# Four matmul tasks behind each layer norm run side by side, contraction outermost

## The chip, the cores and the metric

The kernel runs on one core of a Trainium2 chip. The metric is the device time of one execution in microseconds (us). Before the change three runs gave 1962.46, 1962.93 and 1963.6 us (median 1962.93). The profiled execution took 1963.4 us, and its recorded span is 1961.5 us.

## The reference, cut to what matters

One inference step of a two-layer decoder. 592 tokens (16 meta tokens, 8 x 8 sample tokens, 512 prompt tokens) of width 1024 go through two layers. Every layer is a mixer (recurrent heads), a layer norm, a squared-ReLU MLP and a second layer norm:

```python
def _layer_norm(x, g, b):
    mu = jnp.mean(xf, -1, keepdims=True)
    var = jnp.mean(jnp.square(xf - mu), -1, keepdims=True)
    return (xf - mu) * lax.rsqrt(var + LN_EPS) * g + b

def _sq_relu_mlp(h, w1, w2):
    return jnp.square(jax.nn.relu(h @ w1)) @ w2

for layer in range(DEPTH):
    mixed, states = mixer(h, ...)             # layer 0: SSD and RG-LRU, layer 1: GLA and HGRN
    h = _layer_norm(ALPHA * h + mixed, ln1_g, ln1_b)
    h = _layer_norm(ALPHA * h + _sq_relu_mlp(h, w1, w2), ln2_g, ln2_b)
```

So there are four norms: layer 0's two, layer 1's two. What follows the first and the third is the MLP's first projection; what follows the second is layer 1's input projection (q, k, v of its first GLA head and a low-rank gate); the fourth ends the program.

## The kernel before, in words

Activations lie with the features on the partitions: 8 tiles `h` of 128 features x 592 tokens. A weight unit (`w`) is 1024 x 128: 8 contraction steps of 128 x 128. Each number is held in two float32r parts (a high one and the rest), so a step of a task is three matmuls (high x high, high x rest, rest x high), and a unit on one half of the tokens is 24 matmuls into one PSUM tile `pm` (`mm`, L175). The 592 tokens are two halves of 296 (288 in layer 1 behind its mixer). A `Task` (L263) is a unit with what consumes its two results. `run(..., by_half=True)` (L289) runs some tasks on half 0, then the same tasks on half 1. There are five `pm` banks and three `px` banks of PSUM, five weight buffers `w` and three raw buffers.

A weight unit is loaded by SyncE (SP, L120), its high part is made by ScalarE (ACT, L126) and its rest by VectorE (DVE, L127); `prep_to` (L156) issues this for units up to four ahead.

The norm (`Norm`, L397) works on the residual tiles `rs[0..7]` in halves. The last five tasks ahead of it (j = 3 to 7) run by half. After each result the residual is added on DVE (L519 or L634), `add` (L431) adds the tile to a running sum `s` on GpSimd (POOL; the eighth on DVE; L442, L444), squares it on ACT (L446) and adds the square to `ss` on DVE (L447). `finish(0)` (L449) puts the statistics of half 0 into `later`, a table of functions by contraction step, which `mm` looks up after each step: with FIK = 3 the two matmuls with ones (L463, L465) stand behind step 3 of the first task of half 1. From them come mean and 1/sigma (L466 to L474), the mean is subtracted from the eight tiles (DVE L478, POOL L480), and each tile is scaled on DVE (L494), written to `h` by ACT (L495) and its rest by DVE (L496). `finish(1)` does the same for half 1. The next tasks read the eight `h` in turn.

Behind the second norm POOL adds the bias to the eight `rs` (L645), SP stores them (L646), and behind these stores in SP's queue stand the loads of the next mixer, the small gate weight `wg2` (L1124) first; its matmuls are at L1378.

The order of the instructions on each engine is made by the framework's scheduler when the program is built: it takes what its own model of time finds ready, by priority, and fixes a list for each engine. On the chip every engine works through its list in that order.

Of the kernel before, what the change touches and what calls it, by code (L numbers as in the profile page):

```python
# [12 lines left out]
OP = mybir.AluOpType  # L13

P = 128
D = 1024
KT = 8
# [6 lines left out]
NPM = 5  # L24
NB = 5
SHK = 5
FIK = 3
FINY = (2, 4, 6)
SUBP = (1, 3, 5, 7)
KS = 8 - NB  # L30
# [41 lines left out]
def _trunk(ctx, tc, nc, I, O):  # L72
# [97 lines left out]
    def next_unit():  # L170
        u = state["use"]
        state["use"] += 1
        prep_to(u + 1 + LOOK)
        return prepped.pop(u)
# [94 lines left out]
    def drain():  # L269
        while active or later:  # L270
            for k in sorted(later):
                for fn in later.pop(k):
                    fn()
            weave()

    class Task:
# [6 lines left out]
        def half(self, i):  # L283
# [8 lines left out]
            flush()  # L292
            weave()

    def run(tasks, by_half=False, after=None):
        if by_half:
            for i in range(2):
                for t in tasks:
                    t.half(i)
                if after:  # L300
                    after(i)
        else:
            for t in tasks:
                t.half(0)
                t.half(1)
# [89 lines left out]
    class Norm:  # L395
# [3 lines left out]
        def __init__(self, new, rs, halves, gname, bname, layer, final=False):  # L399
            self.rs, self.halves, self.final = rs, halves, final  # L400
            self.gname, self.bname, self.layer = gname, bname, layer
            self.new = new

        def shift(self):

# [25 lines left out]
        def add(self, k, i):  # L431

            c0, c1 = self.halves[i]
            r = self.rs[k][:, c0:c1]
            if k == KS:
                V.tensor_tensor(r, r, self.c[:, c0:c1], OP.subtract)
            s, ss = self.s[:, c0:c1], self.ss[:, c0:c1]
            if k == 0:
                A.activation(ss, r, AF.Square)
                return  # L440
            if k == 1:
                G.tensor_tensor(s, self.rs[0][:, c0:c1], r, OP.add)  # L442
            else:
                (V if k == KT - 1 else G).tensor_tensor(s, s, r, OP.add)  # L444
            q = self.t[k % 2][:, c0:c1]
            A.activation(q, r, AF.Square)  # L446
            V.tensor_tensor(ss, ss, q, OP.add)  # L447

        def finish(self, i, dst):  # L449
            if i == 0:  # L450
                later.setdefault(FIK, []).append(lambda: step(self.finishing(i, dst)))
            else:
                drain()
                for _ in self.finishing(i, dst):
                    pass

        def finishing(self, i, dst):
            c0, c1 = self.halves[i]
            n = c1 - c0
            gname, bname, layer = self.gname, self.bname, self.layer  # L460
# [86 lines left out]
    def mlp(H, layer, halves, last, keep=None):  # L547
# [3 lines left out]
        with ExitStack() as st:  # L551
# [93 lines left out]
                        G.tensor_scalar(rs[k], rs[k], vc("ln2b", layer * 8 + k), None, OP.add)  # L645
                        nc.sync.dma_start(keep[:, k], rs[k])  # L646

            run([w1(0, f) for f in W1_ORDER[:4]], by_half=True)
            for k, f in enumerate(W1_ORDER[4:]):
                run([w1(0, f)])  # L650
                residual(2 * k)
# [467 lines left out]
    def odd_mixer(H, g):  # L1119
# [266 lines left out]
        for h in range(4):  # L1386
            q, k, v0, v1 = (g(n) for n in ("q", "k", "v", "v"))
            tasks = [copy_task(q, TAIL), copy_task(k, FULL), copy_task(v0, FULL), copy_task(v1, FULL)]
            if h == 0:
                run([Task(H, FULL, lr_consume, small=wsr[:, 1])] + tasks[0:NB], by_half=True)  # L1390
                run(tasks[NB:])
            else:
                run(tasks)
            z = [g("zs"), g("zs")]
            while len(lsg) <= h:
                weave()
            active.append(attend(q, k, lsg[h], 1.0 / 16, P ** -0.5, (v0, v1), z, hg[:, 0:2],
                                 I["gst"][h], O["gla_s"][h], O["gla_p"][h], 1))
            run([silu_task(z[0]), silu_task(z[1])])
# [209 lines left out]
```

## Time and profile before

| what | value |
|---|---|
| median of three runs | 1962.93 us |
| profiled execution, its span | 1963.4 us, 1961.5 us |
| TensorE (PE) busy | 1889.2 us, 96% of the span |
| DVE / ACT / POOL busy | 66% / 45% / 21% |
| chain that ended last | PE 81%, DVE 11%, issue 3% |
| statistics of half 0 of the four norms (L463) start at | 474.82, 886.52, 1528.01, 1930.33 us |
| statistics of half 1 (L463) start at | 499.11, 911.34, 1552.43, 1948.69 us |

Times count from the start of the span. "Busy" is the sum of the instructions' times. The clock that the power and activity control granted to TensorE is given in parts of full speed: 1.00 is 2.4 GHz, 0.50 is 1.2 GHz.

### The profile page before, as it was taken

Reading aid. Unit: us, or ns where it says so; the run is one execution under the profiler, and the core shown is the slowest. Engines: PE = TensorE matmul, PEld = TensorE weight load, DVE = VectorE, ACT = ScalarE, POOL = GpSimd, SP = SyncE. Lnnn points to the kernel's source line nnn. Section 1 sums busy time; section 2 is a strip of 40 time slices with the busy share of each in tenths; the row PEclk is TensorE's granted clock in tenths of the full one; section 3 lists DMA queues with packets and bytes.
Section 4 is the critical chain, followed back from the end, with each engine's and each line's share of the span. In section 5 each row is a group of like instructions: output and inputs, shape, how many; then the busy total and the mean of one; then the engine's idle time right before and its main releaser. Section 6 shows DMA issues by size and latency. Waiting matters only on the chain.

```text
span 1961.5 us, 33567 instructions
## 1 busy us (share of the span) xinstructions
PE 1889.2 (96%) x13854; PEld 1827.5 (93%) x13854; DVE 1299.2 (66%) x2023; ACT 885.0 (45%) x1538; POOL 408.2 (21%) x427
## 2 busy tenths in 40 slices
PE   8998899999999999998999999999999899999996
PEld 8898799899999999997899999999999899999996
DVE  7886756877875757557554456566564877575637
ACT  5333146533644444324544355565651563534333
POOL 3454432215100000135212212122112300000015
PEclk9999899999999999999999999999999999999998
DMA  6222221421213131312332322322332123131411
GB/s 202 90 103 75 78 87 55 131 77 54 87 55 118 56 118 56 118 65 86 114 111 93 107 89 88 100 79 97 102 113 76 54 76 112 61 119 55 129 54 49
DMA packets 69272, 175.96 MB, mean 90 GB/s; under 512 B 6624, under 2 KB 30304, under 8 KB 67968
## 3 DMA queue, kind: packets, MB, share of 16 engines
q1 hardware_dynamic: 69120, 173.82, 26.7%
q8 instruction: 109, 1.79, 0.4%
q14 instruction: 43, 0.35, 0.1%
HBM read 154.54 MB, written 19.25 MB: 89 GB/s over the span
## 4 chain that ended last, share of the span: by engine, by line
PE 81%; DVE 11%; issue 3%; ACT 2%; POOL 2%; DMA 0%; SPq 0%; ACTq 0%; DVEq 0%; POOLq 0%
PE pm L182 55%; PE pm L195 14%; DVE w L127 1%; DVE r L424 1%; PE px L1252 1%; PE px L1312 1%; POOL r L645 1%; PE px L1323 1%; PE px L1065 1%; PE px L1322 1%; PE px L946 1%; POOL o L1347 1%; DVE h L496 1%; DVE r L494 1%; PE px L1253 1%
## 5 line engine op out<-in xcount | busy, mean ns | idle before, releaser
L182 PE MATMUL pm<-h,w 128*128 128x296 f32 (+2 forms) x8256 | 1181.7, 301 | 12.5 <-ACT h L308 5.5
L182 PEld LDWEIGHTS pm<-h,w 128*128 128x128 f32 x8256 | 1135.9, 190 | 24.6 <-issue 5.6
L127 DVE TENSOR_TENSOR w<-raw,w 128x1024 fp32r<-128x1024 f32 (+1 forms) x300 | 370.8, 1236 | 181.9 <-ACT w L126 180.9
L126 ACT CAST w<-raw 128x1024 fp32r<-128x1024 f32 (+1 forms) x300 | 304.0, 1014 | 298.9 <-PE pm L195 148.7
L195 PE MATMUL pm<-ff,w 128*128 128x296 f32 (+1 forms) x2016 | 273.5, 297 | 0.0
L195 PEld LDWEIGHTS pm<-ff,w 128*128 128x128 f32 x2016 | 272.0, 188 | 0.3 <-DVE r L214 0.2
L620 POOL TENSOR_TENSOR sq<-sq 128x296 f32<-128x296 f32 (+1 forms) x32 | 21.5, 674 | 651.7 <-ACT sq L618 651.7
L182 PE MATMUL pm<-ff,w 128*128 128x296 f32 (+1 forms) x768 | 106.7, 301 | 0.0
L182 PEld LDWEIGHTS pm<-ff,w 128*128 128x128 f32 x768 | 105.3, 191 | 0.8 <-issue 0.3
L182 PE MATMUL pm<-m,w 128*128 128x296 f32 (+1 forms) x768 | 105.8, 299 | 0.0
L182 PEld LDWEIGHTS pm<-m,w 128*128 128x128 f32 x768 | 104.5, 189 | 0.6
L607 DVE TENSOR_TENSOR ff<-sq,ff 128x888 fp32r<-128x888 f32 (+3 forms) x48 | 58.4, 1221 | 42.2 <-ACT ff L606 42.2
L588 ACT ACTIVATE sq<-pm 128x296 f32<-128x296 f32 (+1 forms) x96 | 37.9, 415 | 87.0 <-PE pm L182 66.0
L606 ACT CAST ff<-sq 128x888 fp32r<-128x888 f32 (+3 forms) x48 | 50.3, 1050 | 39.6 <-DVE sq L601 38.9
L1347 POOL TENSOR_TENSOR o<-o,zs 128x576 f32<-128x576 f32 x16 | 30.8, 1933 | 168.1 <-DVE o L1346 168.1
L211 DVE TENSOR_TENSOR r<-r,pm 128x296 f32<-128x296 f32 (+1 forms) x96 | 43.5, 453 | 18.6 <-PE pm L195 17.9
L1265 POOL TENSOR_TENSOR sin<-sin,ebl 128x1024 f32<-128x1024 f32 (+1 forms) x12 | 29.6, 2467 | 117.9 <-issue 112.0
L589 ACT ACTIVATE sq<-sq 128x296 f32<-128x296 f32 (+1 forms) x96 | 41.2, 450 | 0.8
L1352 ACT COPY v<-pm 128x296 f32<-128x296 f32 x32 | 12.9, 405 | 60.9 <-PE pm L182 60.9
L495 ACT ACTIVATE h<-r,vec 128x296 fp32r<-128x296 f32 (+1 forms) x48 | 23.9, 536 | 34.7 <-DVE r L494 34.7
L214 DVE TENSOR_TENSOR r<-r,pm 128x296 f32<-128x296 f32 (+1 forms) x72 | 32.6, 452 | 10.2 <-PE pm L195 10.2
L618 ACT ACTIVATE sq<-pm 128x296 f32<-128x296 f32 (+1 forms) x32 | 13.1, 415 | 56.8 <-PE pm L182 53.8
(387 smaller groups left out, 2270.8 us busy)
## 6 DMA issues: line engine op xcount, KB each, us to landing
raw<-in_w_dram SPq DMA_DIRECT2D x252, 512.0 KB, 3.3
sin<-in_sst_dram SPq DMA_DIRECT2D x8, 512.0 KB, 3.6
out_ssd_s_dram<-sin SPq DMA_DIRECT2D x8, 512.0 KB, 3.1
sin<-in_gst_dram SPq DMA_DIRECT2D x4, 1024.0 KB, 7.4
out_gla_s_dram<-sin SPq DMA_DIRECT2D x4, 1024.0 KB, 3.9
sin<-in_hst_dram SPq DMA_DIRECT2D x8, 512.0 KB, 4.1
out_hgrn_s_dram<-sin SPq DMA_DIRECT2D x8, 512.0 KB, 3.5
xt<-in_x_dram SPq DMA_DIRECT2D x16, 148.0 KB, 3.9
```

The lines of the kernel that those rows point to most:

```text
L126: A.copy(w[:, 0, :n], r)
L127: V.tensor_tensor(w[:, 1, :n], r, w[:, 0, :n].bitcast(F32), OP.subtract)
L182: PE.matmul(p[:, :n], w[:, a, ks], xs[k][:, b, c0:c1], start=(k == 0 and i == 0), stop=(k == KT - 1 and i == 2))
L195: PE.matmul(p[:, :n], w[:, a, ks], xs[k][:, b, :n], start=(first and k == 0 and i == 0), stop=(k == 3 and i == 2), skip_group_check=True)
L211: V.tensor_tensor(y, y, p[:, :n], OP.add)
L214: V.tensor_tensor(y, y, p[:, :n], OP.subtract)
L588: A.activation(q, p, AF.Relu)
L589: A.activation(q, q, AF.Square)
L606: A.copy(t[:, 0, a:e, :n], s[:, a + 1:e + 1, :n])
L607: V.tensor_tensor(t[:, 1, a:e, :n], s[:, a + 1:e + 1, :n], t[:, 0, a:e, :n].bitcast(F32), OP.subtract)
L1265: G.tensor_tensor(sin, sin, ebl[:, 0:8].unsqueeze(2).to_broadcast([P, 8, N]), OP.mult)
L1347: G.tensor_tensor(o[v][:, c], o[v][:, c], gate[v][:, c], OP.mult)
```

## The change

Three things change. `together` (new, L295) runs several tasks on one half with the contraction outermost: one PSUM tile for each task, and at each step the three matmuls of every task, then the next step; the results are consumed one after the other at the end. It is used behind the first three norms. The squares are added to `ss` one tile later than before, the last of them in `finishing`. The statistics of half 0 stand behind step 6 instead of 3 (FIK), and `finish(1)` prepares one more weight unit ahead of the norm's second half.

```diff
-FIK = 3
+FIK = 6
+    def together(tasks, i):
+        ps = []
+        for t in tasks:
+            if t.small is None and t.w is None:
+                t.w = next_unit()
+            ps.append(pm())
+        for k in range(KT):
+            ks = slice(k * P, (k + 1) * P)
+            for t, p in zip(tasks, ps):
+                c0, c1 = t.halves[i]
+                if t.small is not None:
+                    ops = [(p[:32], t.small[:, k, :], b) for b in range(2)]
+                else:
+                    ops = [(p, t.w[:, a, ks], b) for a, b in ((0, 0), (0, 1), (1, 0))]
+                for j, (o, w, b) in enumerate(ops):
+                    PE.matmul(o[:, :c1 - c0], w, t.xs[k][:, b, c0:c1], start=(k == 0 and j == 0),
+                              stop=(k == KT - 1 and j == len(ops) - 1))
+            for fn in later.pop(k, ()):
+                fn()
+        for t, p in zip(tasks, ps):
+            c0, c1 = t.halves[i]
+            t.consume(p[:32 if t.small is not None else P, :c1 - c0], c0, c1, i)
+            flush()
+            weave()
             A.activation(q, r, AF.Square)
-            V.tensor_tensor(ss, ss, q, OP.add)
+            self.add_square()
+            self.square = (ss, q)
+        def add_square(self):
+            if self.square:
+                ss, q = self.square
+                V.tensor_tensor(ss, ss, q, OP.add)
+            self.square = None
             else:
+                prep_to(state["use"] + 4)
                 drain()
         def finishing(self, i, dst):
+            self.add_square()
-            run([w1(0, f) for f in W1_ORDER[:4]], by_half=True)
+            ts = [w1(0, f) for f in W1_ORDER[:4]]
+            together(ts, 0)
+            together(ts[:2], 1)
+            together(ts[2:], 1)
-                run([Task(H, FULL, lr_consume, small=wsr[:, 1])] + tasks[0:NB], by_half=True)
-                run(tasks[NB:])
+                ts = [Task(H, FULL, lr_consume, small=wsr[:, 1])] + tasks
+                together(ts[:4], 0)
+                ts[4].half(0)
+                together(ts[:2], 1)
+                together(ts[2:4], 1)
+                ts[4].half(1)
```

No instruction is added or taken away except by this: the lists of the two programs have the same lengths on each engine, and they differ only around the four norms. The line numbers of the changed kernel are higher by 26 to 40: its L311 is a matmul of `together`, L500 and L502 are the statistics (L463, L465 before), L463 is before's L436, L471 its L444, L481 its L447, L507 its L470, L515 its L478, L531 and L533 its L494 and L496, L532 its L495, L625 the MLP's Relu (L588), L1407 and L1392 the copies L1367 and L1352, L1418 its L1378.

TensorE at the start of the MLP behind the first norm, before (`pm_5260` and `pm_5294` are the results of the first two tasks on half 0, `h_4996` to `h_5003` the eight tiles, `w_4896` and `w_4930` the weights, `lns` and `lnq` the sums of half 1):

```order
L182 MATMUL pm_5260<-h_4996,w_4896 128x296 x3
L182 MATMUL pm_5260<-h_4997,w_4896 128x296 x3
L182 MATMUL pm_5260<-h_4998,w_4896 128x296 x3
L182 MATMUL pm_5260<-h_4999,w_4896 128x296 x3
L182 MATMUL pm_5260<-h_5000,w_4896 128x296 x3
L182 MATMUL pm_5260<-h_5001,w_4896 128x296 x3
L182 MATMUL pm_5260<-h_5002,w_4896 128x296 x3
L182 MATMUL pm_5260<-h_5003,w_4896 128x296 x3
L182 MATMUL pm_5294<-h_4996,w_4930 128x296
L463 MATMUL px_5192<-lns_4790,ones_78 128x296
L465 MATMUL px_5194<-lnq_4791,ones_78 128x296
```

The same place now (the eight tiles are `h_4995` to `h_5002`, the four results `pm_5260`, `pm_5266`, `pm_5272`, `pm_5278`, the fourth weight `w_5193`), the last twelve rows up to the second statistics matmul:

```order
L311 MATMUL pm_5266<-h_4996,w_4929 128x296
L311 MATMUL pm_5272<-h_4996,w_4963 128x296 x3
L311 MATMUL pm_5260<-h_4997,w_4895 128x296 x3
L311 MATMUL pm_5266<-h_4997,w_4929 128x296 x3
L311 MATMUL pm_5272<-h_4997,w_4963 128x296 x3
L311 MATMUL pm_5260<-h_4998,w_4895 128x296 x3
L500 MATMUL px_5197<-lns_4790,ones_78 128x296
L311 MATMUL pm_5266<-h_4998,w_4929 128x296 x3
L311 MATMUL pm_5272<-h_4998,w_4963 128x296 x2
L311 MATMUL pm_5278<-h_4995,w_5193 128x296
L311 MATMUL pm_5278<-h_4996,w_5193 128x296
L502 MATMUL px_5199<-lnq_4791,ones_78 128x296
```

Before, 25 matmuls of the new tasks stood ahead of L463, and they read all eight tiles; now 32 stand ahead of L500, and they read four tiles.

DVE at the end of half 1's sums of the same norm, before (L519 adds the result to the residual, `w_5257` and `w_5291` are weight rests):

```order
L519 TENSOR_TENSOR r_4553<-r_4553,pm_5163 128x296
L496 SCALAR_TENSOR_TENSOR h_5002<-r_4485,vec_73,h_5002 128x296
L496 SCALAR_TENSOR_TENSOR h_5003<-r_4553,vec_73,h_5003 128x296
L447 TENSOR_TENSOR lnq_4791<-lnq_4791,lnt_4794 128x296
L444 TENSOR_TENSOR lns_4790<-lns_4790,r_4553 128x296
L447 TENSOR_TENSOR lnq_4791<-lnq_4791,lnu_4795 128x296
L127 TENSOR_TENSOR w_5257<-raw_5255,w_5257 128x1024
L470 SCALAR_TENSOR_TENSOR lnr_4792<-px_5194,lnm_4793 128x296
L478 TENSOR_TENSOR r_4019<-r_4019,lnt_4794 128x296
```

and now:

```order
L556 TENSOR_TENSOR r_4553<-r_4553,pm_5162 128x296
L481 TENSOR_TENSOR lnq_4791<-lnq_4791,lnt_4794 128x296
L471 TENSOR_TENSOR lns_4790<-lns_4790,r_4553 128x296
L127 TENSOR_TENSOR w_5193<-raw_5191,w_5193 128x1024
L481 TENSOR_TENSOR lnq_4791<-lnq_4791,lnu_4795 128x296
L515 TENSOR_TENSOR r_4019<-r_4019,lnt_4794 128x296
L515 TENSOR_TENSOR r_4175<-r_4175,lnt_4794 128x296
L507 SCALAR_TENSOR_TENSOR lnr_4792<-px_5199,lnm_4793 128x296
L515 TENSOR_TENSOR r_4335<-r_4335,lnt_4794 128x296
L515 TENSOR_TENSOR r_4485<-r_4485,lnt_4794 128x296
L127 TENSOR_TENSOR w_5263<-raw_5261,w_5263 128x1024
L531 SCALAR_TENSOR_TENSOR r_4019<-r_4019,vec_73,lnr_4792 128x296
```

The fourth weight's rest now stands between the last addition to `lns` and the last to `lnq`, two subtractions of the mean stand ahead of the variance (L507), and a fifth weight's rest stands ahead of the scaling of half 1.

TensorE ahead of the gate weight behind the second norm, before (`pm_9525` is k on half 1, `pm_9564` and `pm_9603` the two v) ...

```order
L182 MATMUL pm_9525<-h_9062,w_8990 128x296 x3
L182 MATMUL pm_9525<-h_9063,w_8990 128x296 x3
L1378 MATMUL px_9553<-lgf_9334,wg2_9320 128x296
L1378 MATMUL px_9557<-lgf_9334,wg2_9320 128x296
L182 MATMUL pm_9564<-h_9056,w_9024 128x296 x3
```

... and now (`pm_9525` is k, `pm_9526` the first v, `pm_9603` the second v):

```order
L311 MATMUL pm_9525<-h_9062,w_8989 128x296 x3
L311 MATMUL pm_9526<-h_9062,w_9023 128x296 x3
L1418 MATMUL px_9578<-lgf_9339,wg2_9325 128x296
L1418 MATMUL px_9582<-lgf_9339,wg2_9325 128x296
L1418 MATMUL px_9592<-lgf_9339,wg2_9325 128x296
L182 MATMUL pm_9603<-h_9055,w_9252 128x296 x3
```

The 24 matmuls of the first v on half 1 stood behind the first use of the gate weight; they now stand ahead of it.

## Rows read from the trace of the kernel before

**Rows 1.** PE's waits, whole program: us in total, times, longest.

```profile
PE px L463 <- DVE ln L444: 8.1, 3, 3.5
PE px L463 <- DVE lns L444: 6.9, 2, 3.5
...
PE pm L182 <- DVE h L496: 4.6, 4, 1.4
PE px L1214 <- ACT vt L1190: 4.3, 3, 1.5
...
PE px L1378 <- DMA wg<-in_wg_dram: 3.7, 1, 3.7
```

**Rows 2.** Timeline of PE, first norm: start, us, instructions, count, idle before.

```profile
455.50 15.85 PE L182 MATMUL pm<-m,w 128*128 128x296 f32 x114
474.82 0.77 PE L463 MATMUL px<-lns,ones 128*128 128x296 f32 x2 [3.48 <-DVE lns L444]
...
499.11 1.19 PE L463 MATMUL px<-lns,ones 128*128 128x296 f32 x2
...
500.56 14.71 PE L182 MATMUL pm<-h,w 128*128 128x296 f32 x104
```

**Rows 3.** Timeline of DVE, first norm.

```profile
468.77 0.76 DVE L447 TENSOR_TENSOR lnq<-lnq,lnu 128x296 f32<-128x296 f32 x1 [0.52 <-ACT lnu L446]
...
477.78 0.46 DVE L519 TENSOR_TENSOR r<-r,pm 128x296 f32<-128x296 f32 x1 [1.12 <-PE pm L182]
...
498.15 0.45 DVE L444 TENSOR_TENSOR lns<-lns,r 128x296 f32<-128x296 f32 x1
...
498.90 1.21 DVE L127 TENSOR_TENSOR w<-raw,w 128x1024 fp32r<-128x1024 f32 x1
```

**Rows 4.** Timeline of ACT, first norm: the first Relu behind the norm's eight L495.

```profile
511.93 0.71 ACT L588 ACTIVATE sq<-pm 128x296 f32<-128x296 f32 x2
```

**Rows 5.** Timeline of PE, second norm.

```profile
925.41 2.34 PE L247 MATMUL pm<-h,wsr 128*32 128x296 f32 x16
927.59 6.77 PE L182 MATMUL pm<-h,w 128*128 128x296 f32 x48
938.07 2.34 PE L1378 MATMUL px<-lgf,wg 32*128 32x296 f32 x4 [3.71 <-DMA wg<-in_wg_dram]
940.34 5.25 PE L182 MATMUL pm<-h,w 128*128 128x296 f32 x24
945.52 1.26 PE L1378 MATMUL px<-lgf,wg 32*128 32x296 f32 x4
946.71 3.51 PE L182 MATMUL pm<-h,w 128*128 128x296 f32 x24
```

**Rows 6.** Timeline of ACT, second norm: the copy that frees the first bank.

```profile
924.98 0.38 ACT L1367 COPY lgf<-pm 32x296 f32<-32x296 f32 x1
```

**Rows 7.** Timeline of POOL, second norm.

```profile
919.38 11.90 POOL L645 TENSOR_SCALAR r<-r,vec 128x592 f32<-128x592 f32 x6 [2.17 <-DVE h L496]
...
932.03 3.51 POOL L645 TENSOR_SCALAR r<-r,vec 128x592 f32<-128x592 f32 x2
```

**Rows 8.** Timeline of SP's queue, second norm.

```profile
935.98 0.38 SPq L1124 DMA_DIRECT2D wg<-in_wg_dram  x1
```

**Rows 9.** Timeline of DVE, third norm.

```profile
1532.42 0.46 DVE L519 TENSOR_TENSOR r<-r,pm 128x288 f32<-128x288 f32 x1 [1.55 <-PE pm L182]
```

**Rows 10.** Timeline of PE, fourth norm.

```profile
1911.43 15.43 PE L182 MATMUL pm<-ff,w 128*128 128x288 f32 x114
...
1931.73 15.77 PE L182 MATMUL pm<-ff,w 128*128 128x288 f32 x108
```

**Rows 11.** Timeline of DVE, fourth norm.

```profile
1945.37 0.70 DVE L447 TENSOR_TENSOR ln<-ln 128x288 f32<-128x288 f32 x1 [0.57 <-ACT ln L446]
1947.53 0.46 DVE L634 TENSOR_TENSOR r<-r,pm 128x288 f32<-128x288 f32 x1 [1.45 <-PE pm L182]
```

**Rows 12.** PE by stretches of 2 us: length, busy (instructions), granted clock, DMA share, GB/s.

```profile
940.00:942.00 2.00, 2.00 (x8) 0.50 0.89 334
...
1932.00:1934.00 2.00, 2.00 (x9) 0.50 0.00 0
```

More of the change, by code (lines that the diff above doesn't have):

```diff
@@ L446, in add @@
             A.activation(q, r, AF.Square)
-            V.tensor_tensor(ss, ss, q, OP.add)
+            self.add_square()
[4 more added lines that the diff above has]
+                V.tensor_tensor(ss, ss, q, OP.add)
+            self.square = None
         def finish(self, i, dst):
```

## The prediction

> **What bounds the kernel now.** I read the page first: TensorE (PE) is busy for 96% of the span and is 81% of the chain that ended last, so time is won only where PE stands still, or runs at its lower clock. The list of PE's waits comes next [rows 1]. The reader is to see that the norms are most of it: 15.0 us ahead of the statistics L463 (five waits), 4.6 us for `h` from L496, 3.7 us for the gate weight `wg2`. The timelines of PE and of the engines that it waits for then say, norm by norm, what ends last.
>
> At the first norm PE stands 3.48 us ahead of L463, for the last addition to `lns` [rows 2]. The other three norms show the same wait (the list: five waits, none longer than 3.5). It is DVE that is late there: the tiles of half 0 are long done on PE. Behind it DVE works without a pause from 477.78 [rows 3] to the last sums of half 1 at 499. So the new tasks' wait for `h`, and the statistics of half 1, are set by DVE's list. Behind the second norm the wait for `wg2` has another cause: POOL's eight L645 run from 919.38 to 935.5 [rows 7], the load stands behind their stores in SP's queue [rows 8], and PE begins at 938.07 [rows 5].
>
> A wait costs more than its length. After the 3.71 us without work at 934 to 938 the granted clock was 0.50, that is 1.2 GHz [rows 12]: 24 matmuls took 5.25 us, where the next 24 took 3.51, and four L1378 took 2.34 where the next four took 1.26 [rows 5]. That is 1.7 + 1.1 = 2.8 us on top. The fourth norm shows the same behind its wait [rows 12]: 108 matmuls in 15.77 us, against 15.43 / 114 x 108 = 14.6 before it [rows 10], so 1.15 us.
>
> **Part 1: statistics of half 0, four times.** Step 6 instead of 3 puts 9 more matmuls ahead of L463, at 15.85 / 114 = 0.139 us each [rows 2]: 1.25 us. The squares one tile late should take away DVE's waits of 0.52 us for ACT's square [rows 3], four of them at each norm. But DVE's list hardly moves: the scheduler still puts each square's addition ahead of the next residual, since in its own view the square is ready first. Only the fourth tile's residual slips into one such wait and saves the 0.38 us by which these additions follow one another. I count 0.4 for the whole edit, not 2. PE's wait falls from 3.48 to 3.48 - 1.25 - 0.4 = 1.85 us. I take it that the clock then stays at 2.4 GHz, as at the first norm, where the two pieces of L463 behind 3.48 us of waiting took 0.77 us, against 1.19 at 499.11 [rows 2]; the other case is in the range.
>
> At the fourth norm nothing follows but the tail, and DVE waits 1.45 us for PE's last tile there [rows 11]. So the gain reaches the end: 1.65 us at least. With the clock's 1.15 us it would be 2.8, but DVE itself follows after 1.45 + 0.4 and what earlier statistics give it, about 1 us. I take 2.2, between 1.6 and 2.9.
>
> **Part 2: the first and third norm.** With the contraction outermost a tile of `h` is needed every 12 matmuls (1.7 us), not every three. The 4.6 us of waits for L496 go. What is late next is the statistics of half 1: L500 now stands behind 32 matmuls of the new tasks (4.4 us), before it was behind 25. PE gets there at about 493.6 (the statistics of half 0 at 474.4, about 1 us for themselves, 3 + 96 matmuls of half 1, 13.8, then 4.4), and everything queued behind it on PE waits, until DVE has its last addition to `lns`. That came at 498.15 + 0.45 = 498.6 [rows 3]. It comes about 1.1 us sooner: 0.4 from part 1, and the third tile's residual no longer waits 1.12 us for PE [rows 3] (3 matmuls behind the statistics, not 12), of which 0.7 is left, since a weight's rest now stands there and waits for ACT's cast. So L500 starts at 497.5, not 499.11.
>
> Then the banks. Four results of half 0 and the first of half 1 fill the five `pm`. The second result of half 1 needs the first bank, which ACT's first Relu frees, and that stands behind all eight `h` of half 1, before [rows 4] and now. Now PE gets there after 96 + 17 = 113 matmuls, before after 96 + 24 = 120. The chain from the statistics to that Relu starts 1.6 us sooner, and has one weight's rest more, 1.21 us [rows 3]: the Relu starts at 511.93 - 0.4 = 511.5 and the bank is free at about 512.0. At that moment PE has done 113 matmuls. Before, it had 25 + (512.0 - 500.56) x 104 / 14.71 = 106 [rows 2]. Gain: 7 matmuls, 1.0 us. So of 3.48 + 3.3 us of waits at this norm only 1 us comes back; DVE and ACT take the rest.
>
> The third norm has the same lists. There the third tile's residual waited 1.55 us [rows 9], at the lower clock, so DVE wins 1 us more: 2.0 us.
>
> **Part 3: the second norm.** The bank of the gate's copy decides here too: L1367 at 924.98 [rows 6], PE half 1 at 925.41 [rows 5]. DVE's list up to the sums of half 1 has one weight's rest fewer than before, so the eight `h` and this copy come some 1.4 us sooner, and so do POOL's L645 and `wg2`. But ACT's list has the copy of the gate's half 1 ahead of q's: q's second result waits for it after 16 matmuls, about 1.2 us (two copies of 0.38 and two hand-overs). Until `wg2` is needed PE wins only 0.2 us. What counts is the order: 24 matmuls of the first v, half of 48 in 6.77 us [rows 5], 3.4 us, now stand ahead of the first L1378. PE gets there at 927.59 - 0.2 + 6.77 + 3.4 = 937.6, and `wg2` is there 1.4 us before 938.07. The wait is gone: 0.5 us sooner with 3.4 us more done, and no lower clock behind it, 2.8 us. Against this the first head's chain loses its cover: ACT's `vt` copies are waited for at the later heads, 4.3 us in three waits [rows 1]; I take 1.0 for the first. Sum 0.5 + 3.4 + 2.8 - 1.0 = 5.7 us, between 3 and 8.
>
> **The rest.** Three matmuls to one bank and the next three to another are nowhere in the trace for these shapes. The 560 matmuls concerned would cost 1.1 us, or win it, by the difference between two stretches at full clock, 6.77 / 48 = 0.141 [rows 5] and 0.139 us; I take 0. The weight unit prepared earlier moves no load: SP's list is the same word for word; its rest on DVE is counted above.
>
> **Sum.** 2.2 + 1.0 + 2.0 + 5.7 = 10.9 us. The profiled execution took 1963.4 us, which is 1.9 us around its span of 1961.5; so 1952.5, and the median of the three runs lies 0.5 below that execution: 1952.0 us.
>
> **Rivals.**
>
> *The wins stay small (0.20).* DVE and ACT set the end at the first three norms as before, because their lists are as long, and only the moved matmuls count: 3.4 us less 1.0 at the second norm, 1.65 at the fourth, and 0 for the clock, since the new wait ahead of L500 (4 us) and that for a bank lower it as often as the old ones. 4 us: 1959. For it speaks that DVE shows no gap there; against it, that the wait for `wg2` is POOL's and SP's, and there the matmuls really move.
>
> *The queue stands behind the fourth weight (0.05, slower).* PE's list puts the fourth weight's matmuls ahead of L502, and DVE's list its rest ahead of the last square. If DVE's last `lns` is no earlier than before (498.6), L502 comes 1.2 us later than its like, a fifth weight's rest adds 1.2, the Relu starts at 514.3, and PE has done 113 matmuls where before it had 25 + 13.9 x 7.07 = 123: 1.4 us lost, and 1.7 with the lower clock behind a wait of 5 us; at two norms 6 us. At the second norm `wg2` comes 2.4 us later, and the 3.4 us shrink to 1. With 1.65 at the fourth: 1966. It decides from about 0.5 us by which `lns` is late.
>
> *Evacuation in a bunch (0.06, within the noise).* Four results end together, so ACT's Relus come as a block, and PE waits for each bank; with the rows above (0.71 us for two Relus) and the lower clock behind each such wait, 1.7 us, it would cost some 2.5 us at each of three norms: 1952 + 7.5 = 1959.5. The Trainium skill, in "TensorE: Matmul & The Clock Gate", section "Loop structure matters more than you think", calls the opposite nest good: contraction inside one output tile, so that the copy out of one runs under the matmuls of the next. By that rule this change goes the wrong way. The trace agrees that PE has no wait inside such tasks away from the norms; but at the norms the good nest waits too, for `h`.
>
> *All of it comes back (0.09).* 13 us of waits, and the lower clock at five places: 18 us, 1945. Against it stands the bank.
>
> **How the numbers follow.** The forecast has 0.60; its own range, from the bounds of the terms, is 1948 to 1957. With most of the small wins on one side and a part of the full one on the other, 1945 to 1960 holds eight in ten. 0.2% is 3.9 us, about what a measurement tells from no change, so 1959 divides. Faster: 0.60 + 0.09 + half of 0.20 + a third of 0.06 = 0.81. Slower: 0.05. Same: the other halves, 0.14.
>
> **What the new profile would show.** The waits ahead of L500 of half 0 at 1.5 to 2.2 us, not 3.5; no waits for L533; one wait of 3 to 4.5 us ahead of L500 of half 1 at three norms, for L471; a wait for L625 at the first and third norm before matmul 114; no wait for `wg`, with 24 matmuls at about 0.14 us behind it. I would be wrong if `wg` still had a wait over 2 us, if L500 of half 1 began no earlier against the norm's start than L463 did, or if the waits of half 0 were gone altogether.

## The result, and the profile after

Four runs of the changed kernel took 1952.51 to 1953.54 us, median 1953.32; four of the kernel before on the same chip 1962.46 to 1964.19, median 1963.26. The ratio is 0.9948 with a 95% interval of 0.9931 to 0.9966: faster by 9.9 us. Forecast was 1952.0 us, between 1945 and 1960. The sum was met; the ledger under it was not, as the runs below show. The profiled execution took 1953.5 us, with a span of 1951.7. TensorE (PE) was busy for 1885.4 us of it, 3.8 less than before with the same number of matmuls, and stood still for 66.3, 6.0 less: the waits are the larger part of the win, but not the whole.

PE's waits in the changed kernel, whole program (us in total, times, longest), against [rows 1]:

```profile
PE pm L311 <- DVE r L556: 6.4, 5, 1.8
...
PE px L500 <- DVE ln L471: 4.4, 3, 1.5
PE px L1254 <- ACT vt L1230: 4.4, 3, 1.5
PE pm L311 <- DVE r L671: 3.8, 2, 2.4
PE px L500 <- DVE lns L471: 3.0, 2, 1.5
...
PE pm L311 <- ACT sq L625: 1.7, 2, 1.4
```

The waits ahead of the statistics fell from 15.0 to 7.4 us, and that for `wg` is gone from the list. Those for `h` fell from 9.3 to 0.5 us: before, the list has 4.7 us for L495 and at L247 besides the 4.6 for L496 at L182 that the prediction counted. In their place stand 10.2 us for L556 and L671, the additions of the old task's half 1 to `r`: they free banks. The prediction had none of these.

The first norm, PE's timeline (start, us, instructions, count, idle before), against [rows 2]:

```profile
474.73 0.77 PE L500 MATMUL px<-lns,ones 128*128 128x296 f32 x2 [1.50 <-DVE lns L471]
...
492.08 1.32 PE L311 MATMUL pm<-h,w 128*128 128x296 f32 x8 [1.60 <-DVE r L556]
495.15 4.22 PE L311 MATMUL pm<-h,w 128*128 128x296 f32 x18 [1.75 <-DVE r L556]
499.21 0.66 PE L500 MATMUL px<-lns,ones 128*128 128x296 f32 x2
...
512.98 11.06 PE L311 MATMUL pm<-h,w 128*128 128x296 f32 x79 [1.35 <-ACT sq L625]
```

DVE's last addition and ACT's first Relu there, against [rows 3, 4]:

```profile
497.50 0.45 DVE L471 TENSOR_TENSOR lns<-lns,r 128x296 f32<-128x296 f32 x1
```

```profile
512.53 0.70 ACT L625 ACTIVATE sq<-pm 128x296 f32<-128x296 f32 x2
```

DVE ends 0.65 us sooner than before. But PE, in its fixed order, stands 3.35 us for banks and does 18 matmuls in 4.22 us, at 1.2 GHz, ahead of L500 of half 1: it starts at 499.21, no sooner than L463 had (499.11), and the Relu later.

The second norm, PE, against [rows 5]:

```profile
927.55 10.09 PE L311 MATMUL pm<-h,w 128*128 128x296 f32 x72 [0.48 <-ACT lgf L1407]
937.58 1.76 PE L1418 MATMUL px<-lgf,wg 32*128 32x296 f32 x6
939.26 1.35 PE L182 MATMUL pm<-h,w 128*128 128x296 f32 x8
```

SP's queue there, against [rows 8]:

```profile
935.50 0.38 SPq L1164 DMA_DIRECT2D wg<-in_wg_dram  x1
```

72 matmuls stand ahead of the gate's products and not 48, these begin 0.5 us sooner than before, the list shows no wait ahead of them, and the eight matmuls behind them take 0.169 us each and not 5.25 / 24 = 0.219. It was close: the load of `wg2` was issued 0.48 us sooner than before (935.98), not 1.4, and landed at 937.53, just as PE came. The granted clock, against [rows 12] (stretches of 2 us: length, busy time of PE, PEld, DVE, ACT, POOL, the clock, DMA share, GB/s):

```profile
886.00:888.00 2.00, 1.97 (x11) 1.68 (x12) 1.04 (x3) 0.99 (x3) 0.36 (x1) 1.00 0.04 8
906.00:908.00 2.00, 2.00 (x9) 1.85 (x10) 2.00 (x6) 0.70 (x2) 0.76 (x1) 0.50 0.01 4
...
940.00:942.00 2.00, 2.00 (x12) 1.43 (x11) 1.63 (x4) 1.96 (x5) 0.00 (x0) 1.00 0.98 389
```

It is up behind the shorter wait of half 0 and behind the gate's products, and down behind the waits for banks. In the four norms together it was at 0.50 for 27.3 us before and for 17.1 us now. At the fourth norm, against [rows 10]:

```profile
1923.01 0.75 PE L500 MATMUL px<-ln,ones 128*128 128x288 f32 x2 [1.50 <-DVE ln L471]
...
1923.87 13.51 PE L182 MATMUL pm<-ff,w 128*128 128x288 f32 x99
```

99 matmuls in 13.51 us is 0.1365 each, full clock; 108 in 15.77 before.

**Where the time came from.** PE's list has 13854 matmuls in all these programs, and away from the norms the same ones at the same numbers. So the lead of a kernel at a place is the start of a matmul in before less that of the matmul of the same number: for the changed kernel -0.65 us ahead of the first norm (383.80 and 384.45), -0.24 behind it (562.93 and 563.17), 6.52 behind the second (992.48 and 985.96), 5.60 ahead of the third (1443.91 and 1438.31), 6.67 behind it (1710.69 and 1704.02), 9.92 at the last (1949.26 and 1939.34). The differences, worked out so from the one profiled execution of each kernel, the time for which the clock was at 0.50 in the four norms of that execution (27.3 us before), and the medians of all runs:

| kernel | start | norm 1 | norm 2 | heads | norm 3 | norm 4 | us at 0.50 | median us (before on the same chip) | ratio, 95% |
|---|---|---|---|---|---|---|---|---|---|
| forecast | 0 | 1.0 | 5.7 | 0 | 2.0 | 2.2 |  | 1952.0 |  |
| changed | -0.7 | 0.4 | 6.8 | -0.9 | 1.1 | 3.3 | 17.1 | 1953.32 (1963.26) | 0.9931 to 0.9966 |
| e1_step6 | -0.4 | -0.4 | -2.7 | 0 | -1.3 | 2.6 | 27.3 | 1965.63 (1963.91) | 1.0002 to 1.0021 |
| e2_squares | -0.7 | 1.5 | 5.0 | 0 | 1.2 | 2.4 | 13.7 | 1956.41 (1963.91) | 0.9954 to 0.998 |
| e3_together | -0.2 | -1.0 | 3.8 | -0.1 | -0.4 | -1.2 | 34.1 | 1960.78 (1963.91) | 0.9977 to 0.9996 |
| e4_yield | 1.1 | -0.1 | 2.5 | -1.1 | -0.5 | 0.1 | 27.3 | 1962.34 (1963.91) | 0.9987 to 1.0006 |
| f1_plain | -1.3 | 0.4 | 3.1 | 0 | 1.6 | 3.3 | 17.1 | 1956.21 (1963.41) | 0.9946 to 0.9976 |
| f2_step3 | 0.2 | -1.7 | 7.6 | -1.5 | 1.1 | 0.8 | 20.5 | 1956.54 (1963.41) | 0.9949 to 0.9974 |
| f3_mix | -0.4 | -0.2 | 6.8 | -0.1 | 1.9 | 3.3 | 17.1 | 1951.57 (1963.41) | 0.9924 to 0.9953 |
| f4_subp | -0.2 | 3.8 | 5.6 | -1.5 | 2.6 | 3.5 | 6.8 | 1949.04 (1963.41) | 0.9909 to 0.9939 |
| g1_nosq | -1.1 | 0.3 | -1.2 | -1.5 | 1.7 | 1.3 | 23.9 | 1964.26 (1963.21) | 0.9995 to 1.0014 |
| g2_late | -0.1 | 5.3 | 6.9 | -1.2 | 5.8 | 4.6 | 3.4 | 1940.82 (1963.21) | 0.9869 to 0.9902 |
| g3_plain13 | 0.1 | 3.9 | 5.7 | -1.4 | 4.9 | 3.5 | 3.4 | 1945.95 (1963.21) | 0.9897 to 0.9926 |

The start, where the lists are alike, varies by about 1 us either way, and it goes with the clock: there it was at 0.50 for 20.5 us in e4_yield, 27.3 in f1_plain and g1_nosq and 23.9 in the others. So much of one execution is chance. A row need not add up to the median: e2_squares was profiled in the fastest of its five executions, 1954.05 us.

### The profile page after: what moved, and what is told of

The parts are those of the page before. It is cut to its first block, busy times and chain, and to the rows that moved or that the text cites. A ratio compares the mean times of both kernels' runs of the same rounds, so it can differ in the third digit from the quotient of the medians.

```text
span 1951.7 us, 33588 instructions
## 1 busy us (share of the span) xinstructions
PE 1885.4 (97%) x13854; PEld 1825.6 (94%) x13854; DVE 1297.1 (66%) x2023; ACT 883.2 (45%) x1538; POOL 410.3 (21%) x427
## 4 chain that ended last, share of the span: by engine, by line
PE 80%; DVE 12%; issue 3%; ACT 3%; POOL 1%; DMA 0%; SPq 0%; ACTq 0%; DVEq 0%; POOLq 0%
PE pm L182 52%; PE pm L195 14%; PE pm L311 2%; DVE w L127 1%; DVE r L515 1%; DVE r L531 1%; DVE h L533 1%; DVE r L451 1%; PE px L1292 1%; PE px L1352 1%; PE px L1363 1%; PE px L1362 1%; PE px L1105 1%; PE px L986 1%; POOL o L1387 1%
## 5 line engine op out<-in xcount | busy, mean ns | idle before, releaser
L182 PE MATMUL pm<-h,w 128*128 128x296 f32 (+2 forms) x7728 | 1105.9, 301 | 6.1 <-ACT h L334 5.4
L182 PEld LDWEIGHTS pm<-h,w 128*128 128x128 f32 x7728 | 1063.0, 190 | 15.3 <-ACT h L334 5.4
L182 PE MATMUL pm<-ff,w 128*128 128x296 f32 (+1 forms) x768 | 105.0, 298 | 0.0
L182 PE MATMUL pm<-m,w 128*128 128x296 f32 (+1 forms) x768 | 105.0, 298 | 0.0
L182 PEld LDWEIGHTS pm<-ff,w 128*128 128x128 f32 x768 | 103.7, 188 | 0.4
L182 PEld LDWEIGHTS pm<-m,w 128*128 128x128 f32 x768 | 103.7, 188 | 0.4
L311 PE MATMUL pm<-h,w 128*128 128x296 f32 (+1 forms) x528 | 83.2, 315 | 13.0 <-DVE r L556 6.4
L311 PEld LDWEIGHTS pm<-h,w 128*128 128x128 f32 x528 | 78.0, 201 | 17.1 <-ACT h L532 12.1
L625 ACT ACTIVATE sq<-pm 128x296 f32<-128x296 f32 (+1 forms) x96 | 37.4, 413 | 87.2 <-PE pm L182 66.2
L214 DVE TENSOR_TENSOR r<-r,pm 128x296 f32<-128x296 f32 (+1 forms) x72 | 32.6, 453 | 10.2 <-PE pm L195 10.2
L532 ACT ACTIVATE h<-r,vec 128x296 fp32r<-128x296 f32 (+1 forms) x48 | 23.2, 533 | 34.6 <-DVE r L531 34.6
```

The source lines that it names most:

```text
L182: PE.matmul(p[:, :n], w[:, a, ks], xs[k][:, b, c0:c1], start=(k == 0 and i == 0), stop=(k == KT - 1 and i == 2))
L214: V.tensor_tensor(y, y, p[:, :n], OP.subtract)
L311: PE.matmul(o[:, :c1 - c0], w, t.xs[k][:, b, c0:c1], start=(k == 0 and j == 0), stop=(k == KT - 1 and j == len(ops) - 1))
L625: A.activation(q, p, AF.Relu)
```

## The experiments

Each part of the change alone came first, and the place of the 24 matmuls. Line numbers are those of the changed kernel, in e2_squares and e3_together up to four lower (L499 for L500), in e1_step6 and e4_yield those of the kernel before.

**e1_step6.**

```
-FIK = 3
+FIK = 6
```

> The kernel before with the statistics at step 6 instead of 3 and nothing else. In PE's list one product of the gate weight now also stands ahead of 48 matmuls of q and k at the second norm. Theory of the prediction (DVE's and POOL's work sets the end at the first three norms, PE's at the fourth): PE's wait ahead of the statistics falls by 1.25 us at each norm, nothing of it comes back at norms 1 and 3, 2.4 us come back at the fourth (1.25 and the lower clock's 1.15); at the second norm PE now stands for the gate weight from about 927 to 938 with 48 matmuls (6.8 us) still behind it. Sum 1963.3 + 6.8 - 2.4 = 1967.7 us, between 1964 and 1970. Rival (each of the four norms gives back what the step takes from the wait, and the place of one product doesn't matter): 1963.3 - 4 x 1.25 - 1.15 = 1957 us.

1965.63 us, slower by 1.7: the theory's direction, 2 us less than it said. PE's row at the second norm:

```profile
934.44 1.35 PE L1378 MATMUL px<-lgf,wg 32*128 32x296 f32 x2 [7.86 <-DMA wg<-in_wg_dram]
```

One gate product ahead of 48 matmuls costs a wait of 7.86 us. The fourth norm gives 2.6, as said.

**e2_squares.**

```
-            V.tensor_tensor(ss, ss, q, OP.add)
+            self.add_square()
+            self.square = (ss, q)
```

> The kernel before with the squares added one tile late and nothing else (step 3, plain loops). Theory: DVE's list keeps its order but for one place, so DVE is 0.4 to 0.8 us sooner at each norm's first half; nothing of it comes back at norms 1 to 3, the fourth gives 0.4 to 0.8: 1962.7 us, between 1961.5 and 1963.5, and PE's wait ahead of the statistics at 2.7 to 3.1 us. Rival (the four waits of 0.5 us for the squares go at each norm): PE's wait at 1.4 us and, at four norms, 1955 us.

1956.41 us: 7.5 us from the part that the prediction had priced at 0.4. The wait ahead of the statistics is about the theory's, 2.68 to 2.72 us, and the time nearly the rival's, so both had the mechanism wrong. PE at the second norm, first of before, then of this kernel:

```profile
886.52 1.36 PE L463 MATMUL px<-ln,ones 128*128 128x296 f32 x2 [3.48 <-DVE ln L444]
887.67 1.19 PE L465 MATMUL px<-ln,ones 128*128 128x296 f32 x2
```

```profile
884.95 0.77 PE L499 MATMUL px<-ln,ones 128*128 128x296 f32 x2 [2.72 <-DVE ln L471]
885.55 0.66 PE L501 MATMUL px<-ln,ones 128*128 128x296 f32 x2
...
935.11 1.26 PE L1414 MATMUL px<-lgf,wg 32*128 32x296 f32 x4 [1.35 <-DMA wg<-in_wg_dram]
936.30 3.52 PE L182 MATMUL pm<-h,w 128*128 128x296 f32 x24
```

Behind 2.72 us of waiting the clock was still up, behind 3.48 it was not. From the start of the first to the end of the last the two statistics took 1.26 us and not 2.34, and DVE, ACT and then POOL go on from them: a low clock on PE is paid on DVE's chain too. `wg2` was there at 935.11 and not 938.07, with a lead of 0.8 us at that norm's begin 2.15 us sooner, and behind a wait of 1.35 us the clock stayed up (2.8 us, by the rows of the prediction). 2.15 + 2.8 is the 5.0 of the table. But the length of the wait alone does not tell whether the clock falls: at this norm it was low behind 2.27 us in g1_nosq, and in this kernel itself it was low behind 2.68 us at the third.

**e3_together.** The hunks of `together` and of both places that call it, with step 3 and the squares as before, and with the one more weight unit that `finish(1)` prepares.

> The kernel before with the contraction outermost in the four tasks behind the first three norms and nothing else (step 3, squares as before). Theory: nearly all of its win is at the second norm, where 24 matmuls (3.4 us) move ahead of the gate weight and the lower clock behind that wait goes (2.8 us): 5.5 to 6.8 us there; norms 1 and 3 win 0 to 0.5 us each, since DVE's list and the five banks set the end there; the fourth norm as before. 1956.8 us, between 1955.5 and 1958.5. Rival (the waits for h come back, as the change intends): 1.4 to 3.3 us at norms 1 and 3 each besides, 1951 us.

1960.78 us, faster by 3.1, near neither. The second norm gives 3.8 and not 5.5 to 6.8, since the gate's products here have the low clock behind them, after a wait of only 0.50 us (eight matmuls in 1.72 us, below); the first loses 1.0 to waits for L555, the residual, and the fourth, where nothing is changed, 1.2 to the clock.

```profile
940.23 1.72 PE L182 MATMUL pm<-h,w 128*128 128x296 f32 x8
```

**e4_yield.**

```
         def decays():
-            yield
+            yield; yield
```

> The kernel before with one more empty step ahead of the gate's decays, so that the 24 matmuls of the first v on half 1 stand ahead of the first product with the gate weight, as in the changed kernel; loops, step and squares as before. Theory (at the second norm the order of these 24 matmuls is the whole win): the wait for the gate weight goes from 3.7 us to under 0.5, the 24 matmuls behind it take 3.4 us and not 5.25, and 4 to 6.5 us come back: 1958 us, between 1956.5 and 1959.5. Rival (it is the nest: h, the banks and POOL's bias come sooner, and the order alone only shifts the wait): under 1.5 us, 1962.5 us.

```profile
937.06 1.26 PE L1378 MATMUL px<-lgf,wg 32*128 32x296 f32 x4 [0.39 <-DMA wg<-in_wg_dram]
938.25 3.52 PE L182 MATMUL pm<-h,w 128*128 128x296 f32 x24
941.70 1.26 PE L1378 MATMUL px<-lgf,wg 32*128 32x296 f32 x4
...
947.83 0.76 PE L1378 MATMUL px<-lgf,wg 32*128 32x296 f32 x2 [0.88 <-DVE ls L1380]
948.52 5.06 PE L182 MATMUL pm<-h,w 128*128 128x296 f32 x24
```

Both local signs are the theory's: a wait of 0.39 us, and 24 matmuls in 3.52. At the second pair of gate products (941.70, before 945.52) the lead has grown by 3.82 - 1.0 + 3.4 = 6.2 us. But the later heads' decays come later too; PE waits for `ls`, the clock falls (24 in 5.06), and of 6.2 us 2.5 are left at that norm, and in the median 1.6, which its interval doesn't tell from nothing. So the order, as this run makes it, is not the win of the changed kernel; what the 24 matmuls are worth with the later decays left in place, no run shows.

Then each part was taken out of the whole, and what sets the end at the norms was put to the test.

**f1_plain.** The changed kernel without the hunks of `together`, and without the one more weight unit that `finish(1)` prepares.

> The changed kernel with the plain loops of before in place of the contraction outermost; step 6 and late squares stay. Theory A (from the run with the late squares alone: 0.75 us less for DVE ahead of the statistics of half 0 keeps TensorE's clock up there, the statistics then reach DVE 1.1 us sooner, and the load of the gate weight comes 2 us sooner by that): the second norm gives about 5 us, the fourth 3.3, the first and third 1 each, less 0.7 us by which the start differs; 1954 us, between 1952.5 and 1955.5. Theory B (the ledger of the prediction: the second norm's 5.7 us are the moved 24 matmuls and go with the loops): 1959 us.

1956.21 us: theory A's side, though 0.7 us above its range, and 2.9 us slower than the changed kernel, not 5.7. At norms 1 and 3 the plain loops are as good, within what one execution tells (0.4 and 1.6 against 0.4 and 1.1), at the second they lose 3.7:

```profile
937.02 1.26 PE L1418 MATMUL px<-lgf,wg 32*128 32x296 f32 x4 [3.26 <-DMA wg<-in_wg_dram]
938.21 5.06 PE L182 MATMUL pm<-h,w 128*128 128x296 f32 x24
```

**f2_step3.**

```
-FIK = 6
+FIK = 3
```

> The changed kernel with the statistics at step 3 again; late squares and contraction outermost stay. Theory A: PE waits 2.7 us ahead of the statistics (not 1.5) at each norm; the fourth gives 2.4 and not 3.3 us, the second stays at 6 to 7 and the first and third change by less than 0.7: 1954.5 us, between 1953 and 1956. Rival (the step is what keeps the clock up): the statistics at the second norm at 1.2 GHz again (1.3 us and not 0.77), and 1958 us.

1956.54 us. The clock was up at the second norm, so the rival falls; theory A's median is missed by 2, and it is the clock again, now at the fourth norm, behind a wait like that behind which it had stayed up in e2_squares. The second norm, then the fourth, then the fourth in e2_squares:

```profile
887.25 0.77 PE L500 MATMUL px<-ln,ones 128*128 128x296 f32 x2 [2.71 <-DVE ln L471]
...
1923.92 1.33 PE L500 MATMUL px<-ln,ones 128*128 128x288 f32 x2 [2.72 <-DVE ln L471]
...
1925.59 15.46 PE L182 MATMUL pm<-ff,w 128*128 128x288 f32 x108
```

```profile
1922.64 0.75 PE L499 MATMUL px<-ln,ones 128*128 128x288 f32 x2 [2.68 <-DVE ln L471]
```

**f3_mix.**

```
-                later.setdefault(FIK, []).append(...)
+                later.setdefault(FIK if self.gname == "ln2g" else 3, []).append(...)
```

and the plain loops again in the MLP.

> Late squares at every norm; step 6 and the contraction outermost at the second norm, step 6 at the fourth; step 3 and plain loops at the first and third. Theory A (each norm gives what the same form gave alone): 1.5 + 6.8 + 1.2 + 3.3 = 12.8 us less 0.7 at the start: 1951.3 us, between 1950 and 1952.5. Rival (the contraction outermost costs nothing at the first and third norm, the difference there is clock and chance): 1953.3 us, as the changed kernel.

1951.57 us, in theory A's range and 1.8 below the changed kernel; but the intervals of the two overlap, so the rival is not excluded. And the sum came by other terms: norm 1 gave -0.2 and not 1.5 (the clock fell there behind a wait of 2.74 us: 108 matmuls took 16.42 us), norm 3 gave 1.9 and not 1.2.

**f4_subp.**

```
-SUBP = (1, 3, 5, 7)
+SUBP = ()
```

> The changed kernel with all eight subtractions of the mean on DVE, none on POOL. In the changed kernel four of them took 4.12 us on DVE while POOL did its four in 4.23; alone one took 0.45. Theory A (DVE's list sets the end at the norms, and the two engines slow one another): eight take about 3.1 us in a row, DVE is 1.0 us sooner in each half, norms 1 to 3 give 1 to 2 us each and the fourth 1: 1948.5 us, between 1946.5 and 1950.5. Rival 1 (banks and PE's order set the end at norms 1 to 3): the fourth's 1 us alone, 1952.3 us. Rival 2 (the slow rate is DVE's own here): eight at 1.03 us, 4 us more for each half, 1960 us or more.

1949.04 us, theory A's total; both rivals' times are missed. DVE and POOL in the changed kernel, then DVE here:

```profile
479.48 4.12 DVE L515 TENSOR_TENSOR r<-r,lnt 128x296 f32<-128x296 f32 x4
```

```profile
479.04 4.23 POOL L517 TENSOR_TENSOR r<-r,lnt 128x296 f32<-128x296 f32 x4 [0.71 <-ACT lnt L511]
```

```profile
475.68 0.47 DVE L507 SCALAR_TENSOR_TENSOR lnr<-px,lnm 128x296 f32<-128x296 f32 x1 [0.96 <-PE px L502]
...
479.07 1.59 DVE L515 TENSOR_TENSOR r<-r,lnt 128x296 f32<-128x296 f32 x4
...
481.71 1.59 DVE L515 TENSOR_TENSOR r<-r,lnt 128x296 f32<-128x296 f32 x4
```

Four took 4.12 us beside POOL and 1.59 alone: all eight on one engine are sooner done, with a weight's rest between them, than four on each of two. Norm 1 gives 3.4 us more than in the changed kernel: DVE's list did set its end, and the clock, which fell there in the changed kernel, stayed up. The other terms are not theory A's: the third norm gives 1.5 more, the second 1.2 less, and the fourth 0.2 where 1 was said.

**g1_nosq.** The changed kernel with e2_squares' hunk taken back.

> The changed kernel with each square added at once again; step 6 and contraction outermost stay. In PE's list one product of the gate weight then stands ahead of the 72 matmuls of q, k and v at the second norm, as with the step alone. Theory A (the late squares are more than the 0.4 us that the prediction gave them: DVE 0.75 us sooner at every norm, and in the scheduler's own view the gate product no longer first): PE waits 2.25 us ahead of the statistics, the fourth norm gives 2.6 and not 3.3, norms 1 and 3 lose 0.5 to 1.5 each, and at the second PE stands about 8 us for the gate weight with 72 matmuls (10 us) behind it, 3 to 5 us lost against before: 1967 us, between 1963 and 1970. Rival (the prediction's ledger: the squares are worth 0.4 us, at the fourth norm alone): 1954 us.

1964.26 us: without the late squares nothing is left of the win. Of the 10.9 us that it lies above the changed kernel, 8.0 are lost at the second norm. Again a gate product stands first, and PE waits 6.95 us for it ahead of 72 matmuls:

```profile
934.48 1.35 PE L1418 MATMUL px<-lgf,wg 32*128 32x296 f32 x2 [6.95 <-DMA wg<-in_wg_dram]
```

**g2_late.** On top of f4_subp:

```
-later.setdefault(FIK, []).append(lambda: step(self.finishing(i, dst)))
+later.setdefault(7, []).append(lambda: later.setdefault(1, []).append(lambda: step(self.finishing(i, dst))))
```

> The kernel with all eight subtractions on DVE, and the statistics of half 0 nine matmuls later still (behind 30 and not 21 of the next half's). Theory A (PE's wait of 1.5 us ahead of the statistics is only paid at the fourth norm, since DVE sets the end at the others): the wait falls to 0.2 to 0.4 us at each norm, the fourth gives 1.2 us more, norms 1 to 3 within 0.6 of before: 1947.8 us, between 1946.5 and 1949. Rival 1 (with DVE's list shorter PE sets the end): 1.2 us at each norm, 1944.5 us. Rival 2 (DVE's chain waits for the later statistics): 0.3 us lost at each, 1949.5.

1940.82 us, 8.2 below f4_subp and 12.5 below the changed kernel: more than even rival 1 said. The wait ahead of the statistics is 0.27 to 0.31 us, the fourth norm gives 1.1 more, and the others 1.3 to 3.2 more; the 3.2 are the third's, where the clock had fallen in f4_subp. PE's two L500 at the first norm, then DVE there, from the last square on:

```profile
474.16 0.77 PE L500 MATMUL px<-lns,ones 128*128 128x296 f32 x2 [0.27 <-DVE lns L471]
...
494.78 0.77 PE L500 MATMUL px<-lns,ones 128*128 128x296 f32 x2 [0.57 <-DVE lns L471]
```

```profile
475.37 1.22 DVE L127 TENSOR_TENSOR w<-raw,w 128x1024 fp32r<-128x1024 f32 x1
476.51 1.09 DVE L481 TENSOR_TENSOR lnq<-lnq,lnu 128x296 f32<-128x296 f32 x1
477.52 0.45 DVE L507 SCALAR_TENSOR_TENSOR lnr<-px,lnm 128x296 f32<-128x296 f32 x1
```

A weight's rest and a square now stand ahead of the variance L507, where DVE had stood 0.96 us for PE in f4_subp. From the L500 of half 0 to that of half 1 it takes 20.62 us (474.16 to 494.78) and not 22.30 (474.31 to 496.61 in f4_subp). So the later statistics pay where they don't wait for DVE nor DVE for them.

**g3_plain13.** On top of f4_subp, plain loops in the MLP as in f3_mix, and the one more weight unit prepared at the second norm alone.

> The kernel with all eight subtractions on DVE, with plain loops at the first and third norm (contraction outermost at the second alone). Theory A (a tile of h takes DVE two operations, 0.8 us and more with the work between; the plain nest wants one in 0.4 us, the other in 1.7, so once DVE's list is shorter the contraction outermost is worth something): the first and third give 1 to 2 us less each, 1951.5 us, between 1950 and 1953. Rival (as with the longer list, the nest makes no difference there): 1949 us within 1.

1945.95 us: theory A falls, and the rival is too slow by 3. The first norm is the same with either nest (3.9 and 3.8). The third is better here (4.9 and 2.6), but not shown to be so by the nest: ahead of its tasks PE waited 2.14 us in f4_subp and 1.49 here, and only in f4_subp did the clock fall behind that, to 0.50 for 3.4 us. First f4_subp, then this kernel:

```profile
1520.21 0.75 PE L500 MATMUL px<-lns,ones 128*128 128x288 f32 x2 [2.14 <-DVE lns L471]
```

```profile
1519.05 0.75 PE L500 MATMUL px<-lns,ones 128*128 128x288 f32 x2 [1.49 <-DVE lns L471]
```

**g4_banks.**

```
-NPM = 5
+NPM = 6
```

> The changed kernel with six banks for results and two (not three) for the small products; read at the first norm alone, since the heads in between lose a bank. Theory A (PE's waits there, 1.60 and 1.75 us for the residual L556 and 1.35 for the Relu, are for a free bank): the waits for L556 fall under 1 us in sum and that for the Relu goes; a wait for DVE's last addition to lns ahead of L500 of half 1 may stand in their place; the first norm gives 0.5 to 2.5 us more than in the changed kernel. Rival (they are DVE's list under another name): waits of the same sum (4.7 us within 0.7), for lns and h, and less than 0.4 us at that norm.

The whole took 1986.19 us in two runs: the heads, with one bank fewer for their small products, lose more than the norms win. PE at the first norm, which lies 28 us later here:

```profile
519.53 3.39 PE L311 MATMUL pm<-h,w 128*128 128x296 f32 x23 [1.23 <-DVE r L556]
525.45 1.35 PE L500 MATMUL px<-lns,ones 128*128 128x296 f32 x2 [2.53 <-DVE lns L471]
```

The waits for L556 fell from 3.35 to 1.23 us and that for the Relu went; 2.53 us for `lns` came, as theory A has it, and the norm gives 1.8 us and not 0.4. So it was banks, and behind them DVE.

## Why the prediction was right, and where its reasons were not

The total was met, 9.9 us for 10.9, but through errors that cancel.

- **Part 1, the squares: the step that failed.** "I count 0.4 for the whole edit, not 2." Directly it is 0.75 us at each norm (in the changed kernel 1528.01 less 1521.66 less the lead of 5.60, at the third). What was left out is what hangs on it: the clock behind the shorter wait, the statistics that DVE waits for, and the place that the scheduler gives the gate's products. Alone the late squares give 7.5 us; without them the other two parts give none (g1_nosq). Behind the statistics the prediction had taken the clock back at the fourth norm alone, and on PE alone. How much of the 7.5 us is the clock, which is partly chance, stays open.
- **Part 1, the fourth norm: mis-sized.** 3.3 and not 2.2. All of the clock's 1.15 us came back, and 0.75 from DVE; I had taken it that DVE's list would swallow 0.6.
- **Part 1, the step.** Its 1.25 us went off the wait as forecast, 3.48 to 1.50 with the squares' 0.75 (forecast 1.85). Alone it makes the kernel slower (e1_step6).
- **Part 2, the first and third norm: the wrong wait.** Forecast was one wait of 3 to 4.5 us ahead of L500 of half 1, and that L500 started at 497.5. It had none and started at 499.21, which against the kernel's lead of -0.65 us there is 0.55 sooner, where 1.6 was forecast. I had counted four results of half 0 and one of half 1 into five banks, but not the last two results of the task before, which DVE frees late. g4_banks shows it. The wait for the Relu came at matmul 113, where it was expected. The norms gave 0.4 and 1.1 us, not 1.0 and 2.0.
- **Part 3, the second norm: the size right, the cause half.** 6.8 us for 5.7; the loss of 1.0 for the `vt` copies didn't come (4.4 us, 4.3 before). The 24 matmuls stand where the prediction put them, and they had to: `wg2` was there 0.5 us sooner and not 1.4. But f1_plain keeps 3.1 of the 6.8 without them, e2_squares 5.0, and e4_yield, which moves them and puts off the later decays, gives 2.5. Two cures for one wait don't add.
- **Outside the norms** -0.7 at the start, chance by the other kernels, and -0.9 in the heads: the wait of 1.50 us for `e` is in both kernels (1.51 before), but only in the changed one did the clock fall behind it, with 71 matmuls in 10.65 us and not 9.88. The seven kernels of the table that lose 0.9 to 1.5 us in the heads all show this fall behind that wait, and none of the five that lose 0.1 or less. The changed kernel, then the kernel before:

```profile
1421.51 10.65 PE L182 MATMUL pm<-h,w 128*128 128x288 f32 x71
```

```profile
1427.86 9.88 PE L182 MATMUL pm<-h,w 128*128 128x288 f32 x71
```

The rivals: the wins didn't stay small, not all of the waits came back, and the queue did not stand behind the fourth weight (where 514.3 gives 13.7 us and 122 matmuls, not 13.9 and 123; nothing hangs on it). Evacuation in a bunch was nearest in kind: PE's new waits at three norms are for banks, though less for the Relus than for the old task's results. The Trainium skill's rule ("TensorE: Matmul & The Clock Gate", section "Loop structure matters more than you think") wants the contraction inside one output tile. No run here decides for it or against it: at the first norm the nest made no difference, at the third f1_plain is 0.5 us better, less than chance makes of one execution, and the 2.3 us of g3_plain13 there have the clock beside them; at the second the other nest won by its order.

## What to carry to other kernels

Price an edit on the chain that sets the end by what hangs on it, not by its own length: 0.75 us on DVE came with 7.5, since TensorE's clock behind the wait, the next engine's start and a load's issue hung on it. Where two edits cure the same wait, test each alone and each taken out; the sum of the ledger was right here while its lines were not. And look for the idle time of the slowest engine right behind a round trip: moving the matmuls that it waits for so far back that it has other work meanwhile (g2_late) won 8.2 us, nearly as much as the whole change.

## What the runs showed of the hardware

- **The clock is partly chance.** In the kernel before, the changed one and the twelve others there are 56 waits ahead of half 0's statistics. Behind those of 3.4 to 3.5 us the clock fell in 9 of 12, behind those of 2.7 us in 3 of 10, of 2.1 to 2.3 us in 5 of 9, of 1.5 to 1.6 us in 0 of 21, and of 0.3 us in 0 of 4. The three of 3.48 us that left it up are all at the first norm [rows 2]. At other places a wait of 1.50 us (for `e`, in the heads) and one of 0.50 us (for the gate weight, in e3_together) had the low clock behind them. The ten runs of e3_together lie between 1957.5 and 1963.8 us, the five fastest at a mean granted clock of 0.984 to 0.985, the others at 0.981 to 0.983. A few us between single executions of two kernels with such waits say little.
- **POOL's work slows DVE's.** A subtraction with both inputs in SBUF took 0.40 us on DVE alone (four in 1.59) and 1.03 beside POOL's (four in 4.12). The Trainium skill ("SBUF — State Buffer", section "Who interferes with whom") says that such a DVE instruction contends with a GpSimd instruction that reads SBUF, since its second input comes through the shared read interface. The two traces agree for DVE's side; what POOL loses, no run here shows.
